# Modulation products moved from TensorE to VectorE in a two-block transformer kernel, with smaller edits to norms, scores and load order

## The chip, the cores and the metric

The program runs on one core of one Trainium2 chip, in float32 throughout, and is launched once. The metric is device time in microseconds (us), the median of three runs. "PE" is TensorE, "DVE" VectorE, "ACT" ScalarE, "SP" the engine that issues nearly all loads.

## What is computed

Two blocks of a transformer run one after the other on 256 tokens of width 1024, each with two layers.

- First block, per layer: `h += 0.5*swiglu(rms(h))`, a mixer of three parts (latent attention with rotary scores, a bidirectional mLSTM, a Fourier mixer), a second half-weighted feed-forward, and a gated embedding ("ple"). All feed-forwards have 1024 -> 2816 -> 1024 channels.
- Second block, per layer: feed-forward, mixer, feed-forward, on the 256 tokens and on 256 context tokens together. Here each norm is modulated by the condition vectors `c` and `c_ctx`:

```
mx = (silu(c)     @ ada_w[i] + ada_b[i]).reshape(3, 3, 1, d)
mc = (silu(c_ctx) @ ada_w[i] + ada_b[i]).reshape(3, 3, d)
x  = x + 0.5 * mx[0, 2] * swiglu(rms(x) * g * (1 + mx[0, 1]) + mx[0, 0], w1, w2)
```

So there are 2 layers x 9 vectors of 1024 numbers for each of two conditions. Three vectors (shift, scale, gate) make one modulated part, and layer 0 has parts 0, 1 and 2. They depend on no other data of the program, so they can be made at any time before the part that reads them. The second block's mixers are a gated delta net (layer 0) and window attention (layer 1).

## The kernel before, in words

**Matmuls in three terms.** Every large product is done as hi*hi + lo*hi + hi*lo. `weight` (L143) loads a 128x1024 tile of weights on the SP queue into `raw` (3 buffers), and for each half of it ACT rounds the high part (`whi`, L139) and DVE subtracts for the low part (`wlo`, L140); there are five half-tiles of each. `mm3` (L165 to L167) issues the three matmuls. Activations are split in the same way into `xh` and `xl`.

**A feed-forward** (`ffn`) takes the hidden channels in parts: 8, 7 and 7 tiles where one stream of 256 tokens is in work (`n == 1`: four of them in the first block, one at the end), 6, 6, 5 and 5 where two streams are joined (`n == 2`: three of them). For each part it makes gate and up ("gu"), tile by tile, and then adds the part's down projection ("dn") to the residual in eight steps `m`, one DVE operation each (L408). In each part the gate tile and the up tile are each 8 x 3 matmuls of 256 columns for `n == 1`.

**Modulations of layer 0, parts 0 and 1** are made on PE: `ada` (L468) is called six times. Each call loads eight 512 KB pieces of `ada_w` (tile `adaw`, in the pool of `raw` weights of a chain of its own) and for each does four matmuls at `tile_position=(0, 32*i)`, that is with 32 stationary columns each in four column groups of the array (L476); then come a copy, two transposes and an addition. A float32 matmul shows as two records in the profile, so the 192 instructions are 384 records. `self.tc.cur_priority` is set to multiples of `SPREAD`, which spreads the six calls over the whole first block: the scheduler puts their instructions between those of the feed-forwards and mixers.

**The other modulations** (layer 0 part 2, and all of layer 1) are made by DVE and ACT in `conditions` (L417). A row of `ada_w` sums over 1024 inputs: DVE multiplies a 128x1024 tile by the broadcast condition (L436) and ACT sums each row with its accumulator (L437); two such products, one per condition, for each loaded tile. `conditions` is a generator that `ffn` advances from `aside`: a pace per gate-up tile adds to a credit, and each whole credit issues one step after the last ordered instruction (`issue_after`). It is used beside the three joined feed-forwards.

**A norm.** `rstds` sums the squares over channels with PE (`sums`, L220: for each of two blocks of 128 tokens, two matmuls against a column of ones, for the two halves of the accumulator), takes a reciprocal root on DVE, and spreads the result over partitions with `row_bcast` (L872), a float32 matmul against the identity.

**Rotary scores** (`mla`, L592): heads lie two to a 128-row tile, so the rotary part of the score is a matmul over 64 rows (`r:r + 64`), added to the 128-row part (L591) in the same accumulator.

The order of the work is a scheduler's: each instruction has a priority from its place in the program, changed by `cur_priority`; each engine then runs its list in order. Loads stand in SP's list in that order too.

## Time and profile before

| | before |
|---|---|
| median of 3 runs | 3128.57 us (3128.12 to 3136.78) |
| the profiled execution, its own time | 3128.45 us |
| its span, first to last instruction | 3126.5 us |
| PE busy | 3071.3 us, 98% |
| DVE busy | 2282.5 us, 73% |
| ACT busy | 1748.7 us, 56% |
| mean granted TensorE clock | 0.991 of full speed |
| HBM read | 432.28 MB |

Busy is the union of an engine's instructions, so PE at 98% says that it is seldom empty, and nothing about how densely it is filled: matmuls overlap. How dense they are is read from the distance between the starts of two neighbours in the timeline. "Granted clock" is 1.00 at 2.4 GHz and 0.50 at 1.2 GHz.

### The profile page before, as it was taken

Reading aid. Unit: us, or ns where it says so; the run is one execution under the profiler, and the core shown is the slowest. Engines: PE = TensorE matmul, PEld = TensorE weight load, DVE = VectorE, ACT = ScalarE, POOL = GpSimd, SP = SyncE. Lnnn points to the kernel's source line nnn. Section 1 sums busy time; section 2 is a strip of 40 time slices with the busy share of each in tenths; the row PEclk is TensorE's granted clock in tenths of the full one; section 3 lists DMA queues with packets and bytes.
Section 4 is the critical chain, followed back from the end, with each engine's and each line's share of the span. In section 5 each row is a group of like instructions: output and inputs, shape, how many; then the busy total and the mean of one; then the engine's idle time right before and its main releaser. Section 6 shows DMA issues by size and latency. Waiting matters only on the chain.

```text
span 3126.5 us, 54401 instructions
## 1 busy us (share of the span) xinstructions
PE 3071.3 (98%) x20430; PEld 2678.8 (86%) x20430; DVE 2282.5 (73%) x4921; ACT 1748.7 (56%) x3609; POOL 0.2 (0%) x4
## 2 busy tenths in 40 slices
PE   8999999999999989999999999999999999998999
PEld 8978999999889988888877777888888888896999
DVE  7767776877777786566798888767776666677666
ACT  5545654655565564444577767545554454556555
POOL 0000000000000000000000000000000000000000
PEclk9999999999999999999999999999999999999999
DMA  7564456666445544444211111235553444441465
GB/s 240 188 204 138 158 182 207 212 187 184 167 159 185 178 140 128 133 141 130 85 48 42 42 42 35 95 122 168 170 165 111 135 145 150 143 122 45 130 183 167
DMA packets 129720, 437.92 MB, mean 140 GB/s; under 512 B 14512, under 2 KB 18224, under 8 KB 129072
## 3 DMA queue, kind: packets, MB, share of 16 engines
q1 hardware_dynamic: 129456, 434.43, 44.0%
q8 instruction: 161, 2.64, 0.3%
q14 instruction: 103, 0.84, 0.1%
HBM read 432.28 MB, written 1.05 MB: 139 GB/s over the span
## 4 chain that ended last, share of the span: by engine, by line
PE 92%; DVE 4%; ACT 2%; issue 1%; DMA 1%; SPq 0%; ACTq 0%; DVEq 0%
PE gu L165 15%; PE gu L166 15%; PE gu L167 15%; PE dn L165 7%; PE dn L166 7%; PE dn L167 7%; PE proj L166 4%; PE proj L165 4%; PE proj L167 4%; PE ada L476 1%; DVE wlo L140 1%; PE dn_pw L996 1%; PE dn_px L996 1%; PE ms L220 1%; ACT whi L139 1%
## 5 line engine op out<-in xcount | busy, mean ns | idle before, releaser
L139 ACT ACTIVATE whi<-raw 128x512 fp32r<-128x512 f32 (+1 forms) x1398 | 840.2, 605 | 1016.7 <-PE gu L166 512.4
L140 DVE TENSOR_TENSOR wlo<-raw,whi 128x512 fp32r<-128x512 f32 (+1 forms) x1398 | 913.2, 658 | 536.9 <-ACT whi L139 517.2
L165 PE MATMUL gu<-xh,whi 128*128 128x256 f32 (+1 forms) x2800 | 907.2, 324 | 11.7 <-ACT xh L306 8.5
L166 PE MATMUL gu<-xl,whi 128*128 128x256 f32 (+1 forms) x2800 | 907.0, 324 | 0.2 <-DVE xl L307 0.2
L167 PE MATMUL gu<-xh,wlo 128*128 128x256 f32 (+1 forms) x2800 | 905.5, 324 | 0.1
L165 PEld LDWEIGHTS gu<-xh,whi 128*128 128x128 f32 x2800 | 529.9, 189 | 63.7 <-ACT xh L306 10.4
L166 PEld LDWEIGHTS gu<-xl,whi 128*128 128x128 f32 x2800 | 529.3, 189 | 53.0 <-issue 5.4
L167 PEld LDWEIGHTS gu<-xh,wlo 128*128 128x128 f32 x2800 | 529.3, 189 | 50.1 <-issue 3.7
L165 PE MATMUL dn<-hh,whi 128*128 128x256 f32 (+1 forms) x1388 | 444.9, 322 | 1.3
L166 PE MATMUL dn<-hl,whi 128*128 128x256 f32 (+1 forms) x1388 | 444.2, 321 | 0.0
L167 PE MATMUL dn<-hh,wlo 128*128 128x256 f32 (+1 forms) x1388 | 443.0, 320 | 0.0
L165 PE MATMUL proj<-xh,whi 128*128 128x256 f32 (+2 forms) x936 | 305.2, 329 | 7.1 <-ACT lora_raw L550 1.9
L166 PE MATMUL proj<-xl,whi 128*128 128x256 f32 (+2 forms) x936 | 308.8, 332 | 1.7 <-DVE xl L299 1.6
L167 PE MATMUL proj<-xh,wlo 128*128 128x256 f32 (+2 forms) x936 | 307.0, 330 | 1.5 <-DVE wlo L140 1.5
L165 PEld LDWEIGHTS dn<-hh,whi 128*128 128x128 f32 x1388 | 260.3, 188 | 27.5 <-ACT hh L139 5.8
L166 PEld LDWEIGHTS dn<-hl,whi 128*128 128x128 f32 x1388 | 260.5, 188 | 24.5 <-DVE hl L140 2.9
L167 PEld LDWEIGHTS dn<-hh,wlo 128*128 128x128 f32 x1388 | 260.4, 188 | 21.1
L436 DVE TENSOR_TENSOR ada_t<-ada_w,ada_c 128x1024 f32<-128x1024 f32 x192 | 226.2, 1219 | 0.0
L437 ACT ACTIVATE ada_t<-ada_t 128x1024 f32<-128x1024 f32 x192 | 201.2, 1049 | 29.9 <-DVE ada_t L436 29.5
L165 PEld LDWEIGHTS proj<-xh,whi 128*128 128x128 f32 (+1 forms) x936 | 176.2, 189 | 19.0 <-issue 5.5
L167 PEld LDWEIGHTS proj<-xh,wlo 128*128 128x128 f32 (+1 forms) x936 | 177.1, 189 | 12.3 <-DVE wlo L140 2.2
L166 PEld LDWEIGHTS proj<-xl,whi 128*128 128x128 f32 (+1 forms) x936 | 176.9, 189 | 11.3 <-DVE xl L299 2.5
(524 smaller groups left out, 3754.1 us busy)
## 6 DMA issues: line engine op xcount, KB each, us to landing
raw<-in_ffn_gate SPq DMA_DIRECT2D x176, 512.0 KB, 3.6
raw<-in_ffn_up SPq DMA_DIRECT2D x176, 512.0 KB, 3.5
ada_w<-in_ada_w SPq DMA_DIRECT2D x96, 512.0 KB, 3.5
raw<-in_ffn_down SPq DMA_DIRECT2D x80, 448.0 KB, 3.3
adaw<-in_ada_w SPq DMA_DIRECT2D x48, 512.0 KB, 4.7
raw<-in_ffn_down SPq DMA_DIRECT2D x40, 512.0 KB, 3.6
raw<-in_ffn_down SPq DMA_DIRECT2D x48, 384.0 KB, 3.2
raw<-in_dn_w SPq DMA_DIRECT2D x32, 512.0 KB, 3.5
```

The costliest lines, as they stand in the source:

```text
L139: self.nc.scalar.activation(hi, src, AF.Copy)
L140: return self.nc.vector.tensor_tensor(lo, src, hi.bitcast(F32), op=ALU.subtract)
L165: self.nc.tensor.matmul(out, ah, bh, start=first and i == 0, stop=False)
L166: self.nc.tensor.matmul(out, ah, bl, start=False, stop=False)
L167: self.nc.tensor.matmul(out, al, bh, start=False, stop=last and i == n - 1)
L220: self.nc.tensor.matmul(ms[:, i, b:b + 1], acc[:, j, b * P:(b + 1) * P], self.ones[:, :1], start=j == 0, stop=j == 1)
L436: V.tensor_tensor(p, w, c[:, s], op=ALU.mult)
L437: G.activation(p, p, AF.Copy, accum_out=sums[:, j, k, s:s + 1])
L476: nc.tensor.matmul(ps[32 * i:32 * i + 32], self.cond[:, k], raw[:, i], start=k == 0, stop=k == KD - 1, tile_position=(0, 32 * i))
L996: nc.tensor.matmul(out[:, c], lhs[:, c], rhs[:, c], start=more is None, stop=True, skip_group_check=more is not None)
```

## The change

Three vectors of layer 0 part 0 now come from `conditions` beside the four feed-forwards of the first block, and the six of parts 1 and 2 beside the first joined feed-forward. With `n == 1`, `aside` is called only from the down projections, except the last one of a feed-forward, at a pace of 0.95 a step; with an initial credit of minus three paces this gives 12 steps for each of the four feed-forwards, and each step is now one product for one condition (before: two). The joined feed-forward's pace goes from 0.9 steps of two products to 3.5 of one per gate-up tile; in the two later ones the products per tile stay as they were. `ada_prepare` and `ada` go, and with them the matmuls on column groups.

Further: `row_bcast` is a transpose; ten norms add the accumulator's halves on DVE first and need half of the matmuls on ones (`joined`); the rotary keys are laid out over 128 rows with zeros, so that the rotary score is a 128-row matmul; the first weights and `x` go ahead of the constants on SP, `small` goes on ACT's queue; and 16 matmuls on a tile of ones run before the first weights come.

```diff
-SPREAD = 1700
+WARM = 16
...
+        with self.x.on():
+            warm = self.x.psum([P, P], "warm")
+            for _ in range(WARM):
+                nc.tensor.matmul(warm, self.ones, self.ones, start=True, stop=True)
+        with self.early(-2000):
+            self.small = self.load_const("small", queue=nc.scalar)
...
-    def sums(self, accs):
+    def sums(self, accs, joined=False):
         ms = self.ch.psum([P, len(accs), 2], "ms")
+        n = 1 if joined else 2
         for i, acc in enumerate(accs):
+            if joined:
+                self.nc.vector.tensor_tensor(acc[:, 0], acc[:, 0], acc[:, 1], op=ALU.add)
             for b in range(2):
-                for j in range(2):
+                for j in range(n):
...
+    def early(self, rank=-1000):
+        old, self.tc.cur_priority = self.tc.cur_priority, rank
+        yield
+        self.tc.cur_priority = old
...
         if load:
-            first.append(self.weight(gate_w[0]))
-            load()
-            first.append(self.weight(up_w[0]))
+            with self.early():
+                first.append(self.weight(gate_w[0]))
+                load()
+                first.append(self.weight(up_w[0]))
...
             for j in range(width):
-                aside()
+                if n > 1:
+                    aside()
...
                 if not last:
-                    aside(width / 16)
+                    aside(width / 16 if n > 1 else 1.0)
...
-    def conditions(self, *wanted):
+    def conditions(self, pool, *wanted):
...
             for k in range(KD):
-                w = ch.loc([P, D], "ada_w", bufs=2)
-                nc.sync.dma_start(out=w, in_=self.A["ada_w"][9 * layer + 3 * i + j - 6, k])
+                w = tile([P, D], "ada_w", 2)
+                nc.sync.dma_start(out=w, in_=self.A["ada_w"][9 * layer + 3 * i + j, k])
                 for s in range(2):
-                    p = t[:, s]
+                    p = w if s else tile([P, D], "ada_t", 1)
                     V.tensor_tensor(p, w, c[:, s], op=ALU.mult)
                     G.activation(p, p, AF.Copy, accum_out=sums[:, j, k, s:s + 1])
-                yield
+                    yield
...
-    def ada(self, j, mod):
-        ps = ch.psum([P, 256], "ada")
-        for k in range(KD):
-            raw = ch.w.tile([P, 4, 256], F32, tag="raw", name="adaw", bufs=ch.raw_bufs)
-            nc.sync.dma_start(out=raw, in_=self.A["ada_w0"][j, k])
-            for i in range(4):
-                nc.tensor.matmul(ps[32 * i:32 * i + 32], self.cond[:, k], raw[:, i], start=k == 0, stop=k == KD - 1,
-                                 tile_position=(0, 32 * i))
...
-        krot = ch.loc([P, S], "krot")
-        self.rope(krot, kr, self.cos, self.sin, self.swap)
+        krot = ch.loc([P, 2, S], "krot")
+        nc.vector.memset(krot, 0.0)
+        turned = ch.loc([P, S], "t1", bufs=6)
+        self.rope(turned, kr, self.cos, self.sin, self.swap)
+        for i in range(2):
+            half = slice(64 * i, 64 * i + 64)
+            nc.scalar.activation(krot[half, i], turned[half], AF.Copy)
...
-                nc.tensor.matmul(s, qr[r:r + 64, h // 2, q], krot[r:r + 64], start=False, stop=True)
+                nc.tensor.matmul(s, qr[:, h // 2, q], krot[:, h % 2], start=False, stop=True)
...
-    def row_bcast(self, out, col, start=True, stop=True):
-        self.nc.tensor.matmul(out, col.to_broadcast((P, P)), self.ident, start=start, stop=stop, skip_group_check=not start)
+    def row_bcast(self, out, col):
+        self.nc.tensor.transpose(out, col.to_broadcast((P, P)), self.ident)
...
-                m = Chain(self, early, "m", 10_000_000, 4, 0, {"ad": (1, "*")})
-                with m.on():
-                    self.ada_prepare()
-                    for i in range(2):
-                        sums = m.tmp([P, 3, KD, 2], "ada_s", bufs=2)
-                        for j in range(3):
-                            self.tc.cur_priority = (3 * i + j + 1) * SPREAD
-                            self.ada(3 * i + j, sums[:, j])
-                        self.modulate(0, i, sums)
+                ada = early.enter_context(self.tc.tile_pool(name="ada", bufs=1))
+                first = self.conditions(ada, *((0, 0, j) for j in range(3)))
+                share = lambda last: (first if last else islice(first, 12), 0.95)
...
-                    acc = self.ffn1("ffn1", l, h, acc, load=None if l else load)
+                    acc = self.ffn1("ffn1", l, h, acc, load=None if l else load, side=share(False))
...
-                    acc = self.ffn1("ffn2", l, h, acc)
+                    acc = self.ffn1("ffn2", l, h, acc, side=share(l))
...
-                                 side=(self.conditions(*((0, 2, j) for j in range(3))), 0.9))
+                                 side=(self.conditions(x.ph, *((0, i, j) for i in (1, 2) for j in range(3))), 3.5))
```

PE's list inside the third gate-up part of the first feed-forward, before (`ada` is the modulations' accumulator, `adaw` their weights):

```order
L165 MATMUL gu<-xh,whi 128x256
L476 MATMUL ada<-adaw,cond 32x256
L166 MATMUL gu<-xl,whi 128x256
L476 MATMUL ada<-adaw,cond 32x256
L167 MATMUL gu<-xh,wlo 128x256
L476 MATMUL ada<-adaw,cond 32x256
L165 MATMUL gu<-xh,whi 128x256
```

and in that part now:

```order
L172 MATMUL gu<-xh,whi 128x256
L173 MATMUL gu<-xl,whi 128x256
L174 MATMUL gu<-xh,wlo 128x256
L172 MATMUL gu<-xh,whi 128x256
L173 MATMUL gu<-xl,whi 128x256
```

The matmuls on column groups, one between each two of the feed-forward's there, are gone.

DVE's list in the middle of the second down projection of the first feed-forward, before (`h_x` is the residual, `dn` the accumulator of one step):

```order
L408 SCALAR_TENSOR_TENSOR h_x<-dn,h_x 128x256
L140 TENSOR_TENSOR wlo<-raw,whi 128x512
L140 TENSOR_TENSOR wlo<-raw,whi 128x384
L408 SCALAR_TENSOR_TENSOR h_x<-dn,h_x 128x256
L140 TENSOR_TENSOR wlo<-raw,whi 128x512
L140 TENSOR_TENSOR wlo<-raw,whi 128x384
```

and now:

```order
L428 SCALAR_TENSOR_TENSOR h_x<-dn,h_x 128x256
L461 TENSOR_TENSOR ada_t<-ada_w,ada_c 128x1024
L147 TENSOR_TENSOR wlo<-raw,whi 128x512
L147 TENSOR_TENSOR wlo<-raw,whi 128x384
L428 SCALAR_TENSOR_TENSOR h_x<-dn,h_x 128x256
L461 TENSOR_TENSOR ada_w<-ada_w,ada_c 128x1024
L147 TENSOR_TENSOR wlo<-raw,whi 128x512
L147 TENSOR_TENSOR wlo<-raw,whi 128x384
```

Behind each residual step of that projection now stands one product, ahead of the next weights' low parts. It is so in the second down projection of all four feed-forwards; the first projection of each has four products, and the third none.

SP's list at the start, before:

```order
L130 DMA small<-in_small 128x518
L130 DMA ident<-in_ident 128x128
L130 DMA swap<-in_swap 128x128
L147 DMA raw<-in_ffn_gate 128x1024
L130 DMA tri<-in_tri 128x256
L130 DMA halves<-in_halves 128x2
L1436 DMA h_x<-in_x 128x512 x4
L147 DMA raw<-in_ffn_up 128x1024
```

and now:

```order
L154 DMA raw<-in_ffn_gate 128x1024
L1433 DMA h_x<-in_x 128x512 x4
L154 DMA raw<-in_ffn_up 128x1024
L137 DMA ident<-in_ident 128x128
L137 DMA swap<-in_swap 128x128
L137 DMA tri<-in_tri 128x256
L137 DMA halves<-in_halves 128x2
```

The first weights and `x` have moved ahead of five constants, and `small` has left this queue.

## Rows read from the trace of the kernel before

**Rows 1.** The page's chain that ended last, shares of the span by engine

```profile
PE 92%; DVE 4%; ACT 2%; issue 1%; DMA 1%; SPq 0%; ACTq 0%; DVEq 0%
```

**Rows 2.** Stretches: length, busy PE, PEld, DVE, ACT, POOL; clock, DMA share, GB/s

```profile
82.20:122.10 39.90, 39.90 (x339) 39.90 (x338) 30.42 (x60) 21.27 (x40) 0.00 (x0) 1.00 0.56 179
142.30:199.60 57.30, 57.30 (x405) 44.78 (x403) 31.04 (x62) 21.64 (x41) 0.00 (x0) 1.00 0.60 202
...
483.10:533.40 50.30, 50.30 (x394) 43.02 (x393) 31.36 (x63) 21.75 (x41) 0.00 (x0) 1.00 0.67 222
122.10:142.30 20.20, 20.07 (x171) 19.87 (x170) 14.30 (x28) 10.09 (x18) 0.00 (x0) 1.00 0.64 184
221.00:353.10 132.10, 126.14 (x932) 110.95 (x931) 98.68 (x300) 77.79 (x175) 0.00 (x0) 0.99 0.46 146
785.40:916.10 130.70, 130.49 (x971) 110.89 (x970) 96.00 (x288) 74.43 (x172) 0.00 (x0) 1.00 0.49 163
1163.30:1531.20 367.90, 367.82 (x1626) 298.50 (x1626) 229.33 (x381) 168.02 (x315) 0.00 (x0) 0.99 0.40 124
1541.00:1986.00 445.00, 440.43 (x3309) 345.83 (x3307) 371.65 (x964) 320.70 (x784) 0.00 (x0) 1.00 0.14 42
```

**Rows 3.** Stretches, only PE's work on tile ada: length, PE busy (records), clock, DMA

```profile
142.30:199.60 57.30, 14.30 (x64) 1.00 0.60 202
483.10:533.40 50.30, 8.55 (x54) 1.00 0.67 222
...
221.00:353.10 132.10, 5.10 (x65) 0.99 0.46 146
...
785.40:916.10 130.70, 10.95 (x105) 1.00 0.49 163
...
sum 837.10, PE 48.35; mean PE 5.37
```

**Rows 4.** Timeline of PE in the first feed-forward: start, us, instruction

```profile
160.47 0.39 PE L166 MATMUL gu<-xl,whi 128*128 128x256 f32 x1
...
161.34 0.39 PE L167 MATMUL gu<-xh,wlo 128*128 128x256 f32 x1
```

**Rows 5.** Timeline of PE in the first mixer

```profile
227.65 1.93 PE L476 MATMUL ada<-adaw,cond 128*32 128x256 f32 x30
231.45 0.39 PE L165 MATMUL proj<-xh,whi 128*128 128x256 f32 x1 [1.87 <-ACT lora_raw L550]
```

**Rows 6.** Groups of the whole program: count | busy us, mean ns | idle before

```profile
L436 DVE TENSOR_TENSOR ada_t<-ada_w,ada_c 128x1024 f32<-128x1024 f32 x192 | 226.2, 1219 | 0.0
L437 ACT ACTIVATE ada_t<-ada_t 128x1024 f32<-128x1024 f32 x192 | 201.2, 1049 | 29.9 <-DVE ada_t L436 29.5
L437 ACT ACTIVATION_READ_ACCUMULATOR ada_t<-ada_t 128x1 f32 x192 | 35.5, 185 | 0.0
```

**Rows 7.** The page's DMA issues: count, KB each, us from issue to landing

```profile
ada_w<-in_ada_w SPq DMA_DIRECT2D x96, 512.0 KB, 3.5
```

**Rows 8.** Timeline of the start, all engines

```profile
2.11 0.43 SPq L147 DMA_DIRECT2D raw<-in_ffn_gate  x1
...
8.47 0.58 PE L165 MATMUL gu<-xh,whi 128*128 128x256 f32 x1 [8.47 <-ACT xh L306]
...
10.08 0.41 PE L166 MATMUL gu<-xl,whi 128*128 128x256 f32 x1
...
10.29 0.41 PE L167 MATMUL gu<-xh,wlo 128*128 128x256 f32 x1
```

**Rows 9.** Timeline of PE at two norms

```profile
18.46 1.05 PE L220 MATMUL ms<-ones,acc 128*128 128x1 f32 x8
...
255.40 0.68 PE L872 MATMUL rbc<-ident,rstd 128*128 128x128 f32 x4 [0.38 <-DVE m L622]
```

**Rows 10.** Timeline of PE at the rotary scores

```profile
302.40 0.59 PE L591 MATMUL s<-kn,qn 128*128 128x256 f32 x2
...
303.55 0.70 PE L591 MATMUL s<-kn,qn 128*128 128x256 f32 x2
```

More of the change, by code (lines that the diff above doesn't have):

```diff
@@ L2 @@
 from contextlib import ExitStack, contextmanager, nullcontext
+from itertools import islice
 import numpy as np
@@ L109, in __init__ @@
         self.x = Chain(self, ctx, "x", 0, 3, 5, {"nm": (1, "*")}, (8, 7, 7), 2)
-        self.small = self.load_const("small")
+        self.ones = self.const.tile([P, P], F32, name="ones")
+        nc.vector.memset(self.ones, 1.0)
+        with self.x.on():
[4 more added lines that the diff above has]
+            self.small = self.load_const("small", queue=nc.scalar)
         self.ident = self.load_const("ident")
@@ L113, in __init__ @@
         self.tri = self.load_const("tri", BF16)
-        self.ones = self.const.tile([P, P], F32, name="ones")
-        nc.vector.memset(self.ones, 1.0)
-        self.zeros = self.const.tile([8, S], F32, name="zeros")
+        self.zeros = self.const.tile([8, 1], F32, name="zeros")
         nc.vector.memset(self.zeros, 0.0)
@@ L243, in twice_normed, with rstds @@
         return bc
-    def rstds(self, accs, width, pre=None, keep=None):
+    def rstds(self, accs, width, pre=None, keep=None, joined=False):
         nc, ch = self.nc, self.ch
         n = len(accs)
-        ms = self.sums(accs)
+        ms = self.sums(accs, joined)
         m = ch.tmp([P, n, 2], f"msq{n}")
@@ L310, in rstd_rows @@
     def rstd_rows(self, acc, keep=None):
-        ps = self.rstds([acc], D, keep=keep)[:, 0]
+        ps = self.rstds([acc], D, keep=keep, joined=True)[:, 0]
         rb = self.ch.loc([P, S], "rb")
@@ L414, in ffn @@
         return naccs
-    def conditions(self, *wanted):
-        nc, ch = self.nc, self.ch
+    def conditions(self, pool, *wanted):
+        nc = self.nc
         V, G = nc.vector, nc.scalar
-        c, t = ch.loc([P, 2, D], "ada_c"), ch.loc([P, 2, D], "ada_t")
+        tile = lambda shape, name, bufs: pool.tile(shape, F32, tag=name, name=name, bufs=bufs)
+        c = tile([P, 2, D], "ada_c", 1)
         nc.sync.dma_start(out=c, in_=self.A["cond"])
-        G.activation(t, c, AF.Tanh, scale=0.5)
-        V.tensor_scalar(t, t, 0.5, 0.5, op0=ALU.mult, op1=ALU.add)
-        V.tensor_tensor(c, t, c, op=ALU.mult)
+        for s in range(2):
+            t = tile([P, D], "ada_t", 1)
+            G.activation(t, c[:, s], AF.Tanh, scale=0.5)
+            V.tensor_scalar(t, t, 0.5, 0.5, op0=ALU.mult, op1=ALU.add)
+            V.tensor_tensor(c[:, s], t, c[:, s], op=ALU.mult)
         for layer, i, j in wanted:
             if j == 0:
-                self.modsums = self.const.tile([P, 3, KD, 2], F32, name=f"ada_s{layer}_{i}")
+                lasting = (layer, i) > (0, 1)
+                shape = [P, 3, KD, 2]
+                self.modsums = self.const.tile(shape, F32, name=f"ada_s{layer}_{i}") if lasting else tile(shape, "ada_s", 2)
             sums = self.modsums
             for k in range(KD):
-                w = ch.loc([P, D], "ada_w", bufs=2)
-                nc.sync.dma_start(out=w, in_=self.A["ada_w"][9 * layer + 3 * i + j - 6, k])
+                w = tile([P, D], "ada_w", 2)
+                nc.sync.dma_start(out=w, in_=self.A["ada_w"][9 * layer + 3 * i + j, k])
                 for s in range(2):
-                    p = t[:, s]
+                    p = w if s else tile([P, D], "ada_t", 1)
                     V.tensor_tensor(p, w, c[:, s], op=ALU.mult)
                     G.activation(p, p, AF.Copy, accum_out=sums[:, j, k, s:s + 1])
-                yield
+                    yield
             if j < 2:
@@ L586, in mla @@
             pt = ch.psum([P, 2, S], "pT")
-            r = 64 * (h % 2)
             for b in range(2):
@@ L660, in mlstm @@
         V.memset(rows, 0.0)
-        parts = ch.loc([72, 2, S], "g_parts", BF16)
+        parts = ch.loc([P, 2, S], "g_parts", BF16)
         V.memset(parts, 0.0)
```

48 lines of the change are left out of this document (13 added, 35 removed).

## The prediction

> **What bounds the kernel now.** I read the chain that ended last first: PE has 92% of it [rows 1], so time comes off only where PE gets less to do or waits less. Then the stretches. A gate-up part of seven tiles is 336 matmuls; undisturbed it takes 39.90 us, that is 0.119 us from one start to the next, with PE and its weight loads busy in all of it [rows 2]. A down part of seven is 168 in 20.20 us, 0.120 each. The reader should see that DVE and ACT have slack in the first (30.42 and 21.27 of 39.90) and less than one may think in the second (14.30 and 10.09 of 20.20, before anything is added). So the feed-forwards run at PE's own rate, and what else is put on PE lengthens them one for one.
>
> The matmuls on column groups are such an addition. The same 336 matmuls take 57.30 us where they stand between them in the first feed-forward and 50.30 in the second [rows 2]. One pair of records between two matmuls moves their starts 0.87 us apart (160.47 to 161.34) instead of 0.12 [rows 4]; where 30 records stand together they take 1.93 us, 0.064 each [rows 5].
>
> The sum is made against the profiled execution, 3128.45 us (1.95 above its span); the median of the runs is 0.1 above that. A measurement of this kernel tells about 0.3%, 9.4 us, from no change.
>
> **1. The column-group matmuls go: -50 us.** The two parts give 57.30 - 39.90 = 17.4 and 50.30 - 39.90 = 10.4, together 27.8 us. PE's work on `ada` is 14.30 and 8.55 us there [rows 3], so each microsecond of it costs 1.22. The whole is 48.35 us [rows 3], so 25.5 are elsewhere, worth at most 31. Of these the second mixer's 10.95 stand in a stretch where PE is never idle (130.49 of 130.70): 13.4 us, of which I take 10, since the mixer has chains of small steps in which DVE or ACT will be late next. The first mixer's 5.10 (6.2 us) stand where PE is idle for 6 us anyway; behind the 30 records PE still waits 1.87 us for ACT [rows 5], so part of them filled a wait: 3. The remaining 9.45 (11.5 us) lie mostly in feed-forwards: 9.5. Sum 27.8 + 10 + 3 + 9.5 = 50. Ends: 59 if none filled a wait, 37 if the mixers give nothing.
>
> The Trainium skill, "TensorEngine Tiling (Array Packing)", Key Properties, says that column tiles execute in parallel, by which four of these cost about one; by that rule alone only some 25 us would be there to win (a rival below). The same list says that a change of tiling mode drains the engine, and rows 4 agree with it: it is the changes that cost here.
>
> **2. The products on DVE and ACT in the four feed-forwards: +10 us.** 48 products of 1.22 us on DVE, each followed by 1.05 + 0.19 us on ACT [rows 6], twelve in each feed-forward: four in the first down part, eight in the second. With eight, DVE has 14.30 + 8 x 1.22 = 24.1 us to do in 20.20, ACT 10.09 + 8 x 1.24 = 20.0. DVE is 3.9 us over, and in its list the product stands ahead of the next tile's low parts, behind which PE waits. Against that, five half-tiles are made ahead, about 6 us of PE's work at 2.5 us a tile, and the next gate-up part has 39.90 - 30.42 = 9.5 us of DVE time free, so that the lag does not carry over. I take 2.5 us for each feed-forward. Ends: 0 (the buffer takes all), and 5 (3.9 and some waiting of two full engines for each other), 20 in all. The loads: 24 of 512 KB here instead of 48, so less to move; but each waits on SP until ACT has freed one of two `ada_w` buffers, with the down weights queued behind it. A landing takes 3.5 us [rows 7], a tile and a half, which the weights made ahead cover; if they don't, that is in the 5.
>
> **3. The joined feed-forward, 96 products instead of 48: +1 us.** DVE gets 229.33 + 58.6 = 288 and ACT 168.02 + 59.5 = 228 of 367.90 us [rows 2], so PE's 367.82 hide it; the cover is gone only if bursts of products hold up a tile's weights. Ends 0 and 4. The two later joined ones keep their rate of products: nothing.
>
> **4. The start: -3 us.** The first weights are issued at 2.11 us and PE begins at 8.47 [rows 8]; at the head of the queue they go about 1.4 us earlier, `x` likewise. The first matmuls stand 0.21 us apart (10.08, 10.29), against 0.12 later, which is what half the clock gives: 24 of a first tile lose 2.2 us. The 16 matmuls on ones run in time in which PE has nothing, and should raise the clock before the weights come. 1.4 + 2.2 is 3.6; I take 3, because the loads are still 2 MB deep. Ends 0 and 5. That the constants come later costs nothing: the identity is first needed at the first norm, which begins at 18.46 us [rows 9].
>
> **5. Norms: -7 us.** Eight records on ones take 1.05 us, four broadcasts 0.68 [rows 9]. Ten norms lose half of the former, 0.5 each, but add one DVE operation to the chain in front; 26 pairs of broadcasts become transposes with one record each, 0.34 saved at best. That is 5 + 9 = 14 if PE is the bound at each; where the chain through DVE is, the addition takes it back. I take half. Ends 2 and 14.
>
> **6. Rotary scores: -3 us.** Two records over 128 rows take 0.59 us after others of that shape and 0.70 after those over 64 rows [rows 10]. 16 scores change shape and back: 16 x 2 x 0.11 = 3.5. Ends 1 and 5. The zeroing and the two copies are DVE's and ACT's, once a layer, beside the mixer's projections.
>
> Sum: -50 + 10 + 1 - 3 - 7 - 3 = -52, so **3128.45 - 52 = 3076 us**. All best ends give 59 + 5 + 14 + 5 = 83 less, 3045; all worst 37 + 0 + 2 + 1 - 20 - 4 = 16 less, 3112.
>
> **The rivals.**
>
> *The removed matmuls were cheap.* If the program's cost of them is that of the runs in which they stand together, 0.064 x 384 = 25 us, the sum is 25 worse: 3101. For it: rows 5. Against it: the two parts of rows 2 alone lost 27.8.
>
> *DVE's product takes PE's place, in part.* Each of 48 products pushes PE by its own 1.22 us: +59 instead of +10, which gives 3125, no change. For it: 24.1 us of work in 20.20. Against it: the 9.5 us free just after, and that the first down parts have only four.
>
> *The product and its sum in series hold PE up, slower.* `ada_t` has one buffer, so a product on DVE waits for ACT's sum of the one before last. Should ACT be held by a full set of `whi`, which only PE frees, DVE stands behind it with the residual steps and low parts in its list, and PE gets the whole 1.22 + 1.24 = 2.46 us a product: 48 x 2.46 = 118 instead of 10, so 3128.45 - 52 + 108 = 3184. It decides from (50 + 3 + 7 + 3 - 1) / 48 = 1.3 us a product. For it: ACT at 20.0 of 20.20. Against it: in the list the same `ada_t` comes back only every second product, 5 us later.
>
> *The clock falls at norms.* A stretch with many transposes might count as rest. The Trainium skill, "TensorE: Matmul & The Clock Gate", Part 4, says that transposes don't count as busy for the clock gate. Against it: 445 us of the delta net, with transposes for every head, ran at 1.00 [rows 2]; that trace does not show the rule at work. One fall costs about 0.01 of the joined feed-forward's 367.90 us, 3.7 [rows 2]; should the ten joined norms each bring one, the sum is 37 worse: 3113.
>
> **How the numbers follow.** Forecast 0.77; cheap matmuls 0.08; products in PE's place, no change, 0.07; in series, slower, 0.05; clock 0.03. Faster: 0.77 + 0.08 + 0.03 = 0.88; same 0.07; slower 0.05. The range runs over the forecast's own ends, cut a little at the worse one, and the first rival lies inside: 3045 to 3108; it leaves out the other three cases, 0.15, and the thin end.
>
> **What would show it.** Right: the third gate-up part of the first feed-forward at 40 us and that of the second too; second down parts of the first-block feed-forwards at 20 to 25 us, with PE's waits there ended by `wlo`; the joined one near 368; the second mixer near 120; 0.12 us spacing from the first weights on. Wrong on item 2: second down parts over 27 us. Wrong on item 1: mixers as long as before, with PE idle in them by as much as was taken out.

## The result, and the profile after

The changed kernel takes **3097.35 us** (median of 4 runs, 3096.62 to 3103.44) against 3130.95 before on the same chip (4 runs, 3128.12 to 3136.78): a ratio of 0.990, 95% interval 0.9888 to 0.9912. That is faster, and inside the range, but it is about 31 us of the forecast 52. The profiled execution took 3096.87 us (its span 3095.1).

The changed kernel's page: the chain that ended last, one of the costliest groups, and `ada_w`'s DMA row:

```profile
PE 89%; DVE 5%; ACT 3%; DMA 1%; issue 1%; SPq 0%; ACTq 0%; DVEq 0%
...
L461 DVE TENSOR_TENSOR ada_t<-ada_w,ada_c 128x1024 f32<-128x1024 f32 x144 | 175.4, 1218 | 6.2 <-DMA ada_w<-in_ada_w 6.2
...
ada_w<-in_ada_w SPq DMA_DIRECT2D x144, 512.0 KB, 3.8
```

PE's share of the chain fell from 92% [rows 1] to 89%, and DVE and ACT took two of the three points. The products cost what they did before (1218 ns, [rows 6]), the landing 3.8 us instead of 3.5 [rows 7].

The changed kernel by stretches (columns: length, busy PE, PEld, DVE, ACT, POOL with counts, granted clock, DMA share, GB/s): the third gate-up parts of the first and second feed-forward, a second down part, the two mixers, the joined feed-forward:

```profile
144.50:184.20 39.70, 39.70 (x337) 39.70 (x337) 31.03 (x62) 22.91 (x44) 0.00 (x0) 1.00 0.68 221
465.40:505.00 39.60, 39.60 (x337) 39.60 (x336) 31.03 (x62) 22.81 (x44) 0.00 (x0) 1.00 0.69 221
122.40:144.50 22.10, 21.84 (x172) 20.69 (x171) 20.99 (x34) 15.71 (x30) 0.00 (x0) 1.00 0.65 200
204.70:332.40 127.70, 119.92 (x856) 111.19 (x855) 99.85 (x302) 78.61 (x177) 0.00 (x0) 0.96 0.39 120
761.80:884.60 122.80, 117.61 (x856) 107.62 (x855) 95.44 (x291) 74.69 (x173) 0.00 (x0) 0.99 0.39 124
1131.70:1499.20 367.50, 367.38 (x1624) 298.38 (x1624) 282.69 (x435) 219.27 (x411) 0.00 (x0) 0.99 0.49 158
```

Against [rows 2]: the third gate-up parts went from 57.30 and 50.30 to 39.7, the plain rate, as forecast. A second down part takes 22.1 instead of 20.20. The joined feed-forward holds 53 us more of DVE's work at the same length (367.50; 367.90 before). But the mixers: PE is idle for 7.8 of 127.7 us in the first and 5.2 of 122.8 in the second, where it was idle for 0.2 of 130.70 [rows 2]. Over the whole first block (both kernels up to the last down matmul of the fourth feed-forward; before, then after):

```profile
0.00:1107.80 1107.80, 1089.96 (x8774) 1024.50 (x8774) 829.56 (x1932) 609.28 (x1231) 0.20 (x4) 1.00 0.58 185
```

```profile
0.00:1078.40 1078.40, 1050.98 (x8360) 1022.66 (x8361) 874.96 (x1981) 653.10 (x1326) 0.20 (x4) 0.99 0.57 179
```

PE's busy time fell by 39 us, its idle time rose from 17.8 to 27.4. Two of the new waits, on PE's timeline of the changed kernel, in the first mixer and at the embedding:

```profile
211.73 0.28 PE L702 MATMUL w<-tri,identb 128*128 128x256 bf16 x1
216.00 0.58 PE L172 MATMUL proj<-xh,whi 128*128 128x256 f32 x1 [3.98 <-ACT lora_raw L542]
...
527.44 0.57 PE L231 MATMUL ms<-ones,acc 128*128 128x1 f32 x4 [1.81 <-DVE acc L228]
531.16 0.58 PE L172 MATMUL ple<-ple_ph,whi 128*128 128x256 f32 x1 [3.14 <-ACT ple_ph L146]
```

Where PE did 30 records of `ada` for 1.93 us and then waited 1.87 [rows 5], it now waits 3.98 for the same copy. And each of the two is followed by a stretch at the lower of the clock's two levels (granted clock 0.50, 1.2 instead of 2.4 GHz):

```profile
215.40:225.60 10.20, 9.60 (x45) 9.60 (x46) 5.32 (x30) 3.68 (x10) 0.00 (x0) 0.50 0.38 121
529.40:536.20 6.80, 5.04 (x23) 5.04 (x24) 1.36 (x5) 2.51 (x6) 0.00 (x0) 0.50 0.02 6
```

In the kernel before, the clock falls at the first of these two places as well, behind the wait of 1.87 us that ends at 231.45 [rows 5], but for 3.3 us. At the second place, where the embedding's projections begin at 558.16 us, it does not fall:

```profile
232.90:236.20 3.30, 3.30 (x19) 3.30 (x17) 0.80 (x3) 1.01 (x2) 0.00 (x0) 0.50 0.99 357
558.20:565.00 6.80, 6.60 (x55) 6.25 (x54) 3.64 (x8) 5.76 (x18) 0.00 (x0) 1.00 0.92 330
```

So in the mixer the changed kernel has a longer wait and, in this execution, a longer fall of the clock. The length of the fall isn't fixed by the wait: three of the runs below (broadcasts by matmul, sums by PE, x first) have nearly the same wait there, 3.73 to 3.96 us, and 3.4 us at half clock behind it.

### The profile page after: what moved, and what is told of

Its sections match the earlier page's. It is cut to its first block, busy times and chain, and to the rows that moved or that the text cites. A ratio compares the mean times of both kernels' runs of the same rounds, so it can differ in the third digit from the quotient of the medians.

```text
span 3095.1 us, 53671 instructions
## 1 busy us (share of the span) xinstructions
PE 3028.9 (98%) x19974; PEld 2672.8 (86%) x19974; DVE 2383.8 (77%) x5017; ACT 1846.0 (60%) x3803; POOL 0.2 (0%) x4
## 4 chain that ended last, share of the span: by engine, by line
PE 89%; DVE 5%; ACT 3%; DMA 1%; issue 1%; SPq 0%; ACTq 0%; DVEq 0%
PE gu L173 15%; PE gu L172 15%; PE gu L174 15%; PE dn L174 7%; PE dn L172 7%; PE dn L173 7%; PE proj L172 4%; PE proj L173 4%; PE proj L174 4%; DVE wlo L147 1%; ACT whi L146 1%; PE dn_pw L993 1%; PE dn_px L993 1%; PE dn_pt L993 1%; PE swa_pt L1347 1%
## 5 line engine op out<-in xcount | busy, mean ns | idle before, releaser
L461 DVE TENSOR_TENSOR ada_t<-ada_w,ada_c 128x1024 f32<-128x1024 f32 x144 | 175.4, 1218 | 6.2 <-DMA ada_w<-in_ada_w 6.2
L461 DVE TENSOR_TENSOR ada_w<-ada_w,ada_c 128x1024 f32<-128x1024 f32 x144 | 175.4, 1218 | 0.6
```

The source lines that it names most:

```text
L461: V.tensor_tensor(p, w, c[:, s], op=ALU.mult)
```

## The experiments

The theory, A: in part of the places that they left, the column-group matmuls had filled waits; without them PE idles there and its clock falls, or stays low for longer, behind the wait. Rivals: the smaller edits cost time (B, F), the transposes let the clock fall (C), the products are dearer than thought (G).

All runs against the kernel before; the span is of the profiled execution. Four executions of the changed kernel had spans from 3094.8 to 3101.6, so a difference of 3 us between two spans is read from its stretch, not from the total. The stretches vary too: over the runs that edit nothing in it, the first mixer takes 125.9 to 127.8 us, the first embedding 37.5 to 40.3, and what follows the first block 2013.7 to 2019.9.

| kernel | median us | ratio, 95% | span us |
|---|---|---|---|
| changed | 3097.35 | 0.9900 (0.9888-0.9912) | 3095.1 |
| before, column-group matmuls out | 3088.08 | 0.9869 (0.9846-0.9892) | 3083.7 |
| changed, broadcasts by matmul | 3096.28 | 0.9888 (0.9870-0.9907) | 3094.4 |
| changed, tables early | 3087.97 | 0.9864 (0.9843-0.9885) | 3086.8 |
| changed, embedding input early | 3091.30 | 0.9878 (0.9854-0.9902) | 3089.9 |
| changed, sums by PE | 3089.48 | 0.9874 (0.9860-0.9887) | 3091.3 |
| changed, products out | 3083.01 | 0.9853 (0.9839-0.9866) | 3083.2 |
| changed, both early | 3082.11 | 0.9850 (0.9836-0.9863) | 3081.7 |
| both early, products spread | 3082.05 | 0.9847 (0.9834-0.9861) | 3081.0 |
| changed, fills | 3090.89 | 0.9871 (0.9850-0.9891) | 3086.3 |
| changed, x first | 3094.55 | 0.9883 (0.9863-0.9903) | 3092.0 |
| early, sums by PE, faster pace | 3090.37 | 0.9867 (0.9847-0.9887) | 3088.6 |
| what had helped, together | **3075.25** | **0.9827 (0.9809-0.9845)** | 3073.4 |

Where the time stands, in us, worked out on each trace from the first and last `gu` and `dn` matmul of each feed-forward (FF; "mix" and "ple", the mixers and the first embedding, are what lies between; "rest" is what follows the fourth):

| | before | matmuls out | products out | changed | both early | together |
|---|---|---|---|---|---|---|
| start | 8.5 | 9.6 | 6.6 | 7.5 | 6.8 | 10.1 |
| FF 1 | 211.3 | 193.0 | 196.2 | 197.1 | 197.6 | 197.4 |
| mix 1 | 133.3 | 131.9 | 127.8 | 127.7 | 120.9 | 119.7 |
| FF 2 | 200.6 | 189.2 | 190.2 | 193.1 | 192.6 | 191.2 |
| ple | 37.2 | 40.3 | 39.9 | 40.3 | 32.6 | 34.1 |
| FF 3 | 193.4 | 190.4 | 193.6 | 196.0 | 196.4 | 191.7 |
| mix 2 | 131.9 | 122.1 | 122.6 | 122.8 | 121.6 | 119.6 |
| FF 4 | 191.7 | 190.3 | 190.5 | 193.8 | 193.2 | 192.3 |
| rest | 2018.7 | 2016.9 | 2015.8 | 2016.7 | 2019.9 | 2017.4 |

**The column-group matmuls alone.** In the kernel before, `ada` makes its rows of zeros. Its 48 loads go with the matmuls, so this run doesn't part the two:

```diff
-        ps = ch.psum([P, 256], "ada")
-        for k in range(KD):
...
-                nc.tensor.matmul(ps[32 * i:32 * i + 32], self.cond[:, k], raw[:, i], ...)
-        nc.scalar.activation(rows, ps, AF.Copy)
+        nc.vector.memset(rows, 0.0)
```

> The kernel before with the 192 column-group matmuls and their 48 loads left out, and nothing else changed, so term 1 of the prediction stands alone (the rows that they make are zeros, so the modulations of layer 0, parts 0 and 1, are not computed). Theory A (where those matmuls stood in the mixers, the embedding and the entries of feed-forwards they filled waits that are there anyway, and behind these waits the granted clock falls): the two third gate-up parts win 27 to 28 us and the second mixer 8 to 10, the other places together nothing or lose a few: 34 to 42 us less than before, with waits of PE for ACT's lora_raw and ple_ph and clock at one half behind them. Rival B (term 1 was right, and the smaller edits of norms, scores and start cost time): the full 50 us less, clock near 1.00 through the first block.

The spans differ by 42.8 us, 0.8 more than theory A's upper end and well short of 50; the interval of the ratio (34 to 48 us) leaves 50 out. The two third gate-up parts gave 17.5 and 10.4 (first two rows below), the second mixer 9.8, the first mixer 1.4, and the embedding took 3.1 **more**. In the third gate-up part DMA has the same share with the loads and without, 0.60. The other rows: the first mixer, and two stretches in it and at the embedding at half clock, in a program that has none of the smaller edits:

```profile
142.60:182.40 39.80, 39.80 (x338) 39.80 (x337) 30.63 (x60) 21.27 (x40) 0.00 (x0) 1.00 0.60 184
463.70:503.60 39.90, 39.90 (x339) 39.90 (x338) 30.71 (x60) 21.27 (x40) 0.00 (x0) 1.00 0.59 186
202.60:334.60 132.00, 123.89 (x869) 110.61 (x867) 99.35 (x300) 78.34 (x175) 0.00 (x0) 0.96 0.37 117
213.10:219.80 6.70, 5.88 (x28) 5.88 (x28) 2.60 (x17) 2.64 (x7) 0.00 (x0) 0.50 0.49 141
527.10:533.80 6.70, 5.45 (x24) 5.19 (x25) 1.55 (x9) 2.25 (x6) 0.00 (x0) 0.50 0.05 20
```

The wait ahead of the first of these is there too:

```profile
213.92 0.58 PE L165 MATMUL proj<-xh,whi 128*128 128x256 f32 x1 [3.70 <-ACT lora_raw L543]
```

That is 3.70 us where the kernel before had 1.93 of `ada` and 1.87 of waiting, 3.80 together: the 30 records had cost nothing there. At the embedding, PE in the kernel before and in this run:

```profile
553.83 1.48 PE L476 MATMUL ada<-adaw,cond 128*32 128x256 f32 x18
556.00 1.06 PE L476 MATMUL ada<-adaw,cond 128*32 128x256 f32 x14
557.73 0.68 PE L872 MATMUL rbc<-ident,rstd 128*128 128x128 f32 x4 [0.66 <-DVE rstd L199]
```

```profile
524.99 0.83 PE L220 MATMUL ms<-ones,acc 128*128 128x1 f32 x6 [0.96 <-ACT acc L205]
527.80 1.19 PE L865 MATMUL rbc<-ident,rstd 128*128 128x128 f32 x4 [1.98 <-DVE rstd L199]
529.54 1.43 PE L165 MATMUL ple<-ple_ph,whi 128*128 128x256 f32 x5 [0.55 <-ACT ple_ph L139]
```

So the wait in the mixer, the idling at the embedding's norm and the fall of the clock behind them come from taking the matmuls away, not from what was put in. The wait of 3.14 us for `ple_ph` in the changed kernel is another matter: it is 0.55 us here.

The trace of the kernel before also shows what the program paid for. A group of eight records there costs no more than a pair, which moved its neighbours 0.87 us apart [rows 4]:

```profile
178.06 0.28 PE L167 MATMUL gu<-xh,wlo 128*128 128x256 f32 x1
178.27 0.64 PE L476 MATMUL ada<-adaw,cond 128*32 128x256 f32 x8
178.84 0.39 PE L165 MATMUL gu<-xh,whi 128*128 128x256 f32 x1
```

Over the whole trace 37 pairs move their neighbours 0.83 us apart on average, 12 groups of eight 0.78, and the one group of 30 moves them 2.14, its wait taken off; without a group it is 0.12. So the price went by the group, that is by the change from one form of matmul to the other and back, and little by the records in it. Added up over all 65 groups it is 52.7 us, of which 42.8 were won. By the stretches of the table it is 25.9 in the two third gate-up parts (27.9 won), 3.9 in the rest of the four feed-forwards (6.2), 12.9 in the second mixer (9.8), but 6.4 in the first mixer (1.4), and 3.7 at the embedding (3.1 lost).

**Broadcasts as matmuls again.**

```diff
-        self.nc.tensor.transpose(out, col.to_broadcast((P, P)), self.ident)
+        self.nc.tensor.matmul(out, col.to_broadcast((P, P)), self.ident, start=True, stop=True)
```

> The changed kernel with the row broadcasts as matmuls against the identity again instead of transposes. Theory A: the stretches at half clock stay where they are (near 215, 529, 570 and 812 us); 0 to 5 us slower than the changed kernel. Rival C (transposes at the norms let the clock fall): these stretches go, some 25 us at half clock fewer, 8 to 12 us faster than the changed kernel.

The span is 0.7 us shorter, and three of the four half-clock stretches are in their places, the first of them 3.3 us long instead of 10.2; the one at 812 us is gone:

```profile
217.50:220.80 3.30, 3.30 (x19) 3.30 (x17) 1.52 (x5) 1.01 (x2) 0.00 (x0) 0.50 0.56 158
528.10:534.80 6.70, 4.13 (x20) 4.11 (x20) 2.25 (x14) 1.78 (x5) 0.00 (x0) 0.50 0.19 72
569.10:572.40 3.30, 3.30 (x18) 3.30 (x17) 3.30 (x16) 0.00 (x0) 0.00 (x0) 0.50 0.67 197
```

Rival C falls: it wanted all four gone and 8 to 12 us. That the first is shorter and the last gone isn't the transposes' doing alone, since the run with x first keeps them and has 3.4 us in the first place, and the run with sums by PE keeps them and has no stretch in the last. The Trainium skill, "TensorE: Matmul & The Clock Gate", Part 4, says that transposes don't count as busy in the same way for the clock gate; this run doesn't show that rule at work. The transposes give nothing that can be measured, although they save PE work (lines view, the changed kernel, then this one):

```profile
L869 PE MATMUL rbc<-ident,rstd 128*128 128x128 f32 x44 | 11.9, 309 | 2.7 <-DVE rstd L206 2.2 <-DVE m L619 0.4
```

```profile
L869 PE MATMUL rbc<-ident,rstd 128*128 128x128 f32 x88 | 17.6, 310 | 4.1 <-DVE rstd L206 3.1 <-DVE rstd L272 0.5 <-DVE m L619 0.4
```

5.7 us less busy, none of it in the time.

**Rotary tables early.** `rope_tables` is called inside the first feed-forward at a priority in its first gate-up part, with its buffers in a pool that closes behind it:

```diff
...
+                    with self.tc.tile_pool(name="rope", bufs=1) if l == 0 else nullcontext() as rp:
+                        if l == 0:
+                            with self.early(ROPE):
+                                self.rope_tables(rp)
+                        acc = self.ffn1("ffn1", ...)
-                    if l == 0:
-                        with x.phase("rope"):
-                            self.rope_tables()
```

> The changed kernel with the rotary tables made during the first gate-up part of the first feed-forward instead of behind it, so that their sine and cosine on ACT do not stand ahead of lora_raw. Theory A: the wait of 4.27 us at 211.73 goes and the clock stays at 1.00 there: the first mixer takes 118 to 122 us instead of 126.9, 5 to 9 us less in all. Rival D (the chain of the norm through DVE and ACT is what holds PE there, whatever ACT does before it): 0 to 2 us less, the clock still falls.

8.3 us less. The first mixer falls from 127.7 to 121.7 us; the 10.24 us from 211.73 on now have PE busy throughout, at 1.00:

```profile
205.90:327.60 121.70, 117.18 (x857) 107.73 (x855) 96.05 (x291) 75.28 (x173) 0.00 (x0) 0.99 0.39 125
211.73:221.97 10.24, 10.24 (x86) 9.88 (x85) 8.14 (x34) 6.04 (x15) 0.00 (x0) 1.00 0.42 144
```

6.0 of the 8.3 are in the mixer (4.2 to 6.1 against the runs that edit nothing there); the other 2.3 are a sum over stretches in which nothing was edited, the embedding's 2.8 among them. Rival D falls.

**Embedding input early.** `ple_load` is called ahead of the second feed-forward, into a pool of its own.

```diff
...
-                            acc = self.ple(l, h, acc, self.ple_load(l, x.ph))
+                            with self.early(self.tc.cur_priority + 900):
+                                p = self.ple_load(l, p0)
...
+                                acc = self.ple(l, h, acc, p)
```

> The changed kernel with the first layer's embedding input (ple_p) loaded ahead of the second feed-forward instead of behind it. Theory A: the wait of 3.39 us for ple_ph goes, and with it the 6.8 us at half clock behind it: the stretch takes 31 to 33 us instead of 38.0, 5 to 7 us less in all. Rival E (the added sum of the accumulator's halves on DVE, 1.81 us of wait, is enough to bring the clock down): the clock still falls there, 2 to 3.5 us less.

5.2 us less, and the embedding alone 7.3 (40.3 to 33.0; 4.5 at least against the runs that edit nothing there), at a clock of 1.00. Rival E's forecast fails, but the addition alone isn't tested by it: the projections now run ahead of the norm, so that PE no longer idles for the 1.81 us behind the addition either.

```profile
523.70:556.70 33.00, 30.84 (x254) 30.08 (x253) 30.34 (x88) 24.35 (x58) 0.00 (x0) 1.00 0.47 152
```

**Both**, the two edits together.

> The changed kernel with both moves, rotary tables and the embedding's input early. Theory A: the two waits are in different stretches, so the gains of the single moves, 8.3 and 5.2 us by the spans of their profiled runs, add up: 12 to 15 us less than the changed kernel, some 3082 to 3085 us. Rival: the granted clock falls elsewhere instead, so that the gains do not add: 5 to 10 us less.

13.4 us less by the spans: 8.3 and 5.2 add up. By the medians it is 15.2, and 9.4 and 6.1 for the single moves.

**Fills: the clock apart from the wait.** `fill` issues matmuls on ones into a spare PSUM buffer.

```diff
+            if layer == 0:
+                self.fill("fill", 12)
             ps = self.project(A["w_in"][layer], 5, x)
...
+        if final is None:
+            self.fill("ple", 10)
         e = self.ple_embed(layer, p)
```

> The changed kernel with matmuls on ones put where PE waits: 12 behind the first two projections of the first mixer, 10 around the first norm of the embedding. They shorten no wait; they only give PE something to do in two of them. Theory A: the waits stay as long (fills included), but the stretches at half clock behind them, 10.2 us at 215 and 6.8 us at 529, go or shrink: 4 to 8 us less than the changed kernel, and together with the pure waits, 4.3 and 3.4 us, that accounts for what the two early moves gave. Rival H (behind the wait ACT and DVE are late anyway, so the slower clock costs nothing): within 1.5 us of the changed kernel.

PE's timeline there, and the windows of the two places:

```profile
212.95 2.84 PE L875 MATMUL fill<-ones 128*128 128x128 f32 x24
...
217.25 0.38 PE L172 MATMUL proj<-xh,whi 128*128 128x256 f32 x1 [1.45 <-ACT lora_raw L542]
```

```profile
215.00:225.20 10.20, 8.71 (x69) 7.87 (x67) 8.29 (x43) 5.67 (x14) 0.00 (x0) 1.00 0.48 156
526.30:533.10 6.80, 4.79 (x41) 4.60 (x40) 2.63 (x11) 3.84 (x12) 0.00 (x0) 1.00 0.05 17
```

The wait is as long as it was (2.84 + 1.45 = 4.29 us of fills and idling), the clock stays at 1.00, and the first mixer takes 124.8 instead of 127.7, the embedding 38.6 instead of 40.3: 4.6 us together, if all of it is the clock. The span is 8.8 shorter (6.5 by the medians); the other 4.2 lie elsewhere, 3.0 of it behind the first block, and aren't explained by this edit. Against the runs that edit nothing there, the mixer wins 1.1 to 3.0 us, while the embedding's 38.6 lies within their 37.5 to 40.3. So the clock's part of the 13.3 us that the early moves won in these two stretches (6.0 + 7.3) is a third at most, and most are the waits themselves. Rival H has the mixer against it, though 1.1 us is within its 1.5; at the embedding it stays open.

**Products out.**

```diff
-                    acc = self.ffn1("ffn1", l, h, acc, load=None if l else load, side=share(False))
+                    acc = self.ffn1("ffn1", l, h, acc, load=None if l else load, side=((), 0))
...
-                    acc = self.ffn1("ffn2", l, h, acc, side=share(l))
+                    acc = self.ffn1("ffn2", l, h, acc, side=((), 0))
```

> The changed kernel with the 48 products beside the four feed-forwards of the first block left out, with their loads (the modulation of layer 0, part 0, is not computed). If term 2 of the prediction was sized right, the down parts go back to 20.2 and 23.0 us and the whole takes 8 to 12 us less than the changed kernel. Theory G (the products and their loads also delay the first weights of the next stretch): 13 us less or more, with the first gate-up part of the third feed-forward at 47 to 48 us.

11.9 us less by the spans, 14.3 by the medians: the total doesn't part term 2's size from rival G. The parts do. The second down parts are back at 20.20 us, with 14.3 us of DVE's work, in the row below; the four of them take 9.2 us less than in the changed kernel. The third feed-forward's first gate-up part still takes 50.5, where G wanted 47 to 48, so rival G falls:

```profile
122.60:142.80 20.20, 20.07 (x171) 19.86 (x170) 14.30 (x28) 10.10 (x18) 0.00 (x0) 1.00 0.64 182
```

**Sums by PE again.**

```diff
-        ps = self.rstds([acc], D, keep=keep, joined=True)[:, 0]
+        ps = self.rstds([acc], D, keep=keep)[:, 0]
...
-        bc = self.rstds([acc], D, joined=True)
+        bc = self.rstds([acc], D)
```

> The changed kernel with the ten joined norms summing both halves of the accumulator on PE again (no addition on DVE ahead of them). By term 5 of the prediction this costs half of 1.05 us at each norm, 2.5 to 5 us slower than the changed kernel. Theory F (the addition stands in the chain of the norm, on DVE's list just where the next weights' parts are made, and PE waits for it): the first gate-up part of the third feed-forward falls from 50.5 to 47 to 48 us, its stretch at half clock at 570 goes, and the sum is 2 to 6 us faster.

3.8 us less by the span, 7.9 by the medians, with more work for PE: theory F. The first block takes 10.2 us less; in the profiled run 6.4 of it are lost again behind it, nearly all where nothing of the edit stands. The third feed-forward's first gate-up part, in the changed kernel and here:

```profile
565.80:616.30 50.50, 48.35 (x390) 47.95 (x391) 40.95 (x93) 27.50 (x54) 0.00 (x0) 0.97 0.57 177
```

```profile
562.50:609.40 46.90, 46.90 (x394) 46.78 (x395) 39.45 (x91) 26.79 (x53) 0.00 (x0) 1.00 0.60 184
```

With the addition, PE does the first matmuls there and then waits for `whi` on ACT:

```profile
568.27 0.39 PE L172 MATMUL gu<-xh,whi 128*128 128x256 f32 x1 [1.99 <-ACT whi L146]
```

That the addition brings this about is shown; by which step of the scheduler it puts ACT's work in that order is not. The two later runs with the sums by PE agree: 48.8 and 47.0 us for this part, where all runs with the addition have 50.2 to 51.3.

**x first.**

```diff
-                first.append(self.weight(gate_w[0]))
                 load()
+                first.append(self.weight(gate_w[0]))
```

> The changed kernel with the four loads of x ahead of the first gate weights on SP's queue. Theory I (the start gained 1 us instead of 3 because PE, once it has its first weights, waits 1.2 and 0.7 us for xh and xl behind x's loads, and the clock falls for 3.4 us behind that): the first gate-up part falls from 50.7 us to 47.5 to 49, 1.5 to 3 us less. Rival: the weights come later by as much as x comes earlier: 0 to 0.5 us less.

3.1 us less. PE begins at 9.7 instead of 7.5 us, and the first gate-up part takes 48.4 instead of 50.7. In the changed kernel PE had begun early and then waited:

```profile
11.44 0.39 PE L172 MATMUL gu<-xh,whi 128*128 128x256 f32 x1 [1.21 <-ACT xh L324]
12.52 0.39 PE L173 MATMUL gu<-xl,whi 128*128 128x256 f32 x1 [0.69 <-DVE xl L325]
```

Begin and part together are 0.1 us better with x first (58.1 against 58.2), so theory I's 2.3 us is real for the part and worth nothing in the end; the other 3 us of the span lie in later stretches, none over 1.8. This run is inconclusive on the total.

**Where the products stand.** Two runs put them beside the gate-up tiles: over all three parts at 0.7 a tile, and over the second and third at 1.15 (here with the sums by PE).

```diff
-                if n > 1:
-                    aside()
+                if n > 1 or part:
+                    aside(1.0 if n > 1 else 1.15)
...
-                    aside(width / 16 if n > 1 else 1.0)
+                    aside(width / 16 if n > 1 else 0.0)
```

> Both moves, and the products of the first block beside the gate-up tiles (0.7 a tile, 12 in each feed-forward) instead of the down steps. In a gate-up part DVE and ACT have 9.5 and 18 us free of 39.9 and a part gets at most five products, 6.1 us on DVE, so these should be hidden: down parts back to 20.2 to 20.6 us, gate-up parts at 39.9 to 40.5, and 5 to 9 us less than with the two moves alone. Rival: the product ahead of wlo in DVE's list holds PE up in a gate-up part too: 0 to 3 us less, or more time.

> Both early moves, the norms summed by PE again, and the products of the first block beside the gate-up tiles of the second and third parts (1.15 a tile, 12 in each feed-forward) but not of the first part. From the spans of the profiled runs: 3081.7 with both moves, less 3.8 for the sums, less 3 to 6 for the products (the run that spread them over all three parts won 6 in the later feed-forwards and lost 6 in the first part of the first, where two of the products' loads and tanh stand between the first weights). 3071 to 3077 us. If the gains overlap, 3078 to 3082.

Both missed. At 0.7 the three later feed-forwards gained 2 us in all (not 6, as the second expectation has it), and the first lost 5.2, in its first gate-up part (55.8 us); by what was not separated. At 1.15 the down parts grew: the second of the first feed-forward takes 26.0 us, at a clock of 0.87:

```profile
123.80:149.80 26.00, 23.33 (x170) 22.84 (x169) 17.26 (x33) 11.29 (x21) 0.00 (x0) 0.87 0.62 197
```

All engines of the same run show why: a product (L462) stands on DVE ahead of the first step (L401) of the part's last hidden tile, and ACT's sum (L463) ahead of its tanh; the down part needs that tile:

```profile
125.01 1.22 DVE L462 TENSOR_TENSOR ada_w<-ada_w,ada_c 128x1024 f32<-128x1024 f32 x1
126.14 0.42 DVE L401 TENSOR_TENSOR xn<-gu,rb 128x256 f32<-128x256 f32 x1
126.83 1.04 ACT L463 ACTIVATE ada_w<-ada_w 128x1024 f32<-128x1024 f32 x1
127.87 0.40 ACT L402 ACTIVATE th<-xn 128x256 f32<-128x256 f32 x1
...
130.81 0.80 PE L173 MATMUL dn<-hh,whi 128*128 128x256 f32 x2 [2.58 <-ACT hh L147]
```

So the 9.5 us that DVE has free in a gate-up part don't hide a product at its end. That a lag doesn't carry over from one part to the next, which the prediction took for the other direction, fails here.

**What had helped, together:** both early moves, x first (whose own gain had stayed open), sums by PE, 0.7 a tile except in the first feed-forward.

> Both early moves, x ahead of the first gate weights, the norms summed by PE again, and the products beside the gate-up tiles at 0.7 a tile in three feed-forwards of the first block but beside the down steps in the first feed-forward. The run before it failed on the pace (at 1.15 a tile a product stood on DVE ahead of the last hidden tile of a part, and PE waited 2.58 us for it at 127.95), which 0.7 did not in the run that spread all. From spans: 3081.7 with both moves, less 3.1 for x, less 3.8 for the sums, less 2 for the pace: 3071 to 3075 us. If the gains overlap (the sums and x change which work stands first on ACT's list in the same places), 3076 to 3081.

3075.25 us: 22 less than the changed kernel, 53 less than before, and its interval (0.9809 to 0.9845) is clear of both; by the span, 3073.4, it is where it was expected. What x first gave in it isn't known: the start and the first gate-up part end at 59.7 us here, at 57.0 with both early moves. The first mixer and the embedding:

```profile
207.50:327.20 119.70, 116.27 (x862) 107.46 (x861) 96.07 (x291) 75.56 (x174) 0.00 (x0) 1.00 0.42 130
518.40:552.50 34.10, 31.61 (x262) 30.91 (x261) 30.00 (x86) 24.54 (x58) 0.00 (x0) 1.00 0.53 158
```

## Why the prediction was right, and where it was not

The direction, the bound and the largest term held; the middle was 21 us too low, and that the time lies in the range owes much to the range's width of 63 us. By the spans, which add up to 31.4, and by the ratios of the table, times 3130 us, which add up to 31.3:

| term | forecast | by spans | by ratios | from |
|---|---|---|---|---|
| 1 column-group matmuls | -50 | -42.8 | -41.0 | before, to matmuls out |
| 3 to 6 joined products, start, norms, scores | -12 | -0.5 | -5.0 | matmuls out, to products out |
| 2 products in four feed-forwards | +10 | +11.9 | +14.7 | products out, to changed |

The two columns differ by up to 4.5 us, and the intervals of matmuls out and products out overlap. Either way, term 1 gave 7 to 9 us less than forecast and terms 3 to 6 together 7 to 12 less, and that is most of the miss.

**Term 1, right in kind, 7 too large.** The third parts (27.9 for 27.8) and the second mixer (9.8 for 10) came as worked out. The steps that failed are "the remaining 9.45 lie mostly in feed-forwards: 9.5", which gave 3.8 once the embedding's 3.1 of loss is set against it, and the 3 for the first mixer, which gave 1.4. The price of those matmuls was not what failed: by the spacing of their neighbours the groups behind that 9.5 cost 9.7 us. What failed is that they stood in waits, at the embedding above all. I had read [rows 5] as a wait in part filled; all 30 records filled it, and behind the longer wait that came in their place the clock stayed low for longer. The fills price the clock at 4.6 us in two places at most. I had the fall of the clock only as a rival through transposes, and given it 0.03; its cause was another. Of the sign that I had set for "wrong on item 1", a mixer as long as before came true for the first one when the matmuls alone were out (131.9 of 133.3 us); PE's idle time in it rose by 2.1 us, less than half of the 5.10 taken out, and its mean clock went from 0.99 to 0.96.

The rule that column groups run in parallel (the Trainium skill, "TensorEngine Tiling (Array Packing)", Key Properties) would have left 25 us to win. 42.8 were won; the drain at a change of mode, from the same list, is the rule that the traces agree with, since a group of eight records costs as much as a pair. The rival "cheap matmuls" (3101) came close to the measured time, but for another reason.

**Term 2, right in kind, 2 to 5 too small:** 11.9 or 14.7 for 10; 9.2 of it in the second down parts, with the waits of PE's weight loads there ended by `wlo`. Neither rival of product in PE's place (59) or in series (118) has anything of it.

**Term 3, right:** 367.5 us with 96 products.

**Term 4, failed:** PE begins 3.0 us earlier (9.6 to 6.6, matmuls out to products out), and the first feed-forward takes 3.2 longer. I had counted the earlier weights and not that `x` is the later of the two. The matmuls on ones did what they were for: the first weights run 0.12 us apart (7.97 and 8.09 in the changed kernel) until the waits of 1.21 and 0.69 us; behind these the clock is at 0.50 for 3.4 us.

**Term 5, failed:** "half of 14". The work did leave PE (5.7 us at the broadcasts), but PE wasn't the bound at the norms; the addition on DVE lengthened the chain that was. Without it the first block takes 10.2 us less in the profiled execution, and the whole 7.9 by the medians. I had the addition only as something that "takes it back", and set the term's worse end at a gain of 2; that end should have been a loss.

**Term 6** wasn't run alone. Mixer 1 gained 4.1 from the smaller edits together, mixer 2 lost 0.5. On PE the scores gave more than the 3 forecast: from the first record of a group of them to the next instruction behind it, all 64 records take 18.7 us with the matmuls out and 13.8 with the products out. What of these 4.9 us reached the total stays open.

## What to carry to other kernels

Work that a scheduler has spread over a program also fills its waits: before it is priced by what it costs in a dense stretch, look at what PE would wait for in each place once it is gone, and move those loads and side computations earlier in the same edit. A wait of PE can cost more than its length when the clock falls behind it (4.27 us in the first mixer were worth 4.2 to 6.1), so a short chain at the entry of a stage deserves the trouble of an early load. Small matmuls of another form are best put in few groups: here the price went by the group. Taking work off an engine that is busy 98% of the time wins nothing where a dependent chain runs through another engine, and an operation added to that chain can cost more than the work that it saves.

## What the runs showed that I had not expected

- Waits of PE of 3.98 and 3.14 us were followed by 10.2 and 6.8 us at half clock, waits of 3.73 to 3.96 in the same place of other runs by 3.4; with matmuls on ones in the wait the clock stayed at 1.00, though PE still idled for 1.45 and 2.01 us behind them.
- A group of eight column-group records moved its neighbours no further apart than a pair (0.78 and 0.83 us).
- The same matmuls that cost 17.5 us in one gate-up part saved 3.1 at the embedding (0.3 against the fastest run that edits nothing there).
